# Four seven-product pairs instead of two in the gate and short-convolution blocks of a decoder trunk

## The chip, the cores and the metric

The kernel runs on one core of one Trainium2 chip. The metric is device time in microseconds (us) of one execution, here the median of three runs. All inputs and outputs are float32 in HBM.

## The reference

One layer of a hybrid decoder trunk, 256 tokens, width 2048. After a layer norm, one large projection feeds three token mixers and three gates; the mixers' outputs are projected, gated, summed, projected once more, and a SwiGLU FFN follows. Cut to what matters:

```
x = layer_norm(x, ln_in_g, ln_in_b)
z = einsum('bsd,de->bse', x, w_in)                      # 2048 -> 13312
a_b, a_c, a_h, b_u, b_v, c_a, c_g, g = split(z)         # seven of 1024, g of 3 x 2048
gates = sigmoid(g + gate_bias)
y_a = a_b * causal_conv(a_c * a_h, conv_a_w)            # 3 taps
y_b = chunked_spatial_gating(b_u, b_v, ...)
y_c = silu(layer_norm(causal_conv(c_a * sigmoid(c_g), cc_conv_w) + cc_conv_b))   # 31 taps
merged = sum_n gates[n] * (y_n @ w_branch[n])           # each 1024 -> 2048
x = layer_norm(alpha * x + merged @ w_out)
x = layer_norm(alpha * x + (silu(x @ w_g) * (x @ w_u)) @ w_ffn_out)
```

## The kernel before

**Precision.** Every float32 operand of a matrix product is split in two parts of a shorter format, `hi` (a cast on ScalarE, L127) and `lo` (the difference, on VectorE, L129). A *product* is three matmuls on TensorE, each of 128 x 128 weights and 512 moving columns: hi by hi, lo by hi, hi by lo (`product`, L236 to L238; in the chunk form L190 to L192).

**Weights.** All weight tiles stand in one list, `plan`, in the order of use: 128 rows by 1024 columns (or 256 rows by 512), 512 KB each. `pump` runs at the head of every step: it loads up to DMA_AHEAD tiles ahead into five raw buffers (`wraw`), splits up to SPLIT_AHEAD ahead (`split_one`) into the rings `whi` and `wlo` of SPLIT_BUFS = 7 buffers each, and pops two items of `background`, the list that holds the 248 taps of branch C's convolution (`tap`, L547 and L550). The framework that builds the program may put instructions of one engine into another order than the code's, as far as the data allow; on the chip each engine then runs its instructions in that fixed order.

**Blocks.** `gemm_block` makes 256 tokens by 1024 columns: two token halves by two column halves, four results in four PSUM banks. A step of kind "one" takes a tile of 128 rows through four products. A step of kind "pair" takes two tiles (2 by 2 sub-blocks b11, b12, b21, b22 of 128 x 512) through seven products instead of eight, after Strassen and Winograd: sums of the four token sub-blocks (`token_sums`, in `xTS`, `mTS`, `hS`) against sums of the four weight sub-blocks (`split_pair`: t1 = b11 + b12, t2 = t1 + b22, t3 = b12 + b22, t4 = t2 + b21). Four of the products gather in banks of their own (p1, p5, p6, p7) over all pairs of the block and are added to the results at the end (L281 to L285, then `total`, L644). While these banks are in use, deferred work that needs a bank waits (`run_deferred(held)`).

`add_block` lays out a block's steps: `lead` single tiles first (LEAD = 6, or all there are), then each pair followed by a share of the remaining singles. X_PAIRS = 2 is the number of pairs where the left side is the normalized input; H_PAIRS = 2 in the FFN's second product; S_PAIRS = 3 in the FFN's first.

**Order of the work.** Eight chunk products (branch C's input, branch B's input), then gate blocks `("g", n, b)` of 16 row tiles each followed by a branch product `("p", n, b)` of 8 single tiles; between branch B and branch A stand the three short-convolution blocks ac, ah, ab. So: gB0 pB0 gB1 pB1, ac ah ab, gA0 pA0 gA1 pA1, gC0 pC0 gC1 pC1, then the output block o0 (`("o", 0)`), two output chunks, and the FFN. The deferred tasks of ab (`later`, L755 on) run in the first steps of gA0; `finish_c`, which reads branch C's convolution, runs in gC0.

The pair's split, as it stands:

```
add(ts[:, 0, :], b11, b12)
add(b12, b12, b22)
add(ts[:, 1, :], ts[:, 0, :], b22)
second = split_tile(t1)
add(ts[:, 2, :], ts[:, 1, :], b21)
low = split_tile(ts[:, 0:2, :])
first = split_tile(t0)
last = split_tile(ts[:, 2:3, :], 1)
```

Of the kernel before, what the change touches and what calls it, by code (L numbers as in the profile page):

```python
# [24 lines left out]
NW = 512  # L25
KT = 2
RAW_BUFS = 5
SPLIT_BUFS = 7
DMA_AHEAD = 6
SPLIT_AHEAD = 3  # L30
DEFER = 2
# [7 lines left out]
S_PAIRS = 3  # L39
H_PAIRS = 2  # L40
SUMS_AT = 5
X_PAIRS = 2
LEAD = 6

OFF_AB, OFF_AC, OFF_AH = 0, DA, 2 * DA
OFF_BU, OFF_BV = 3 * DA, 4 * DA
OFF_CA, OFF_CG = 5 * DA, 6 * DA
OFF_G = 7 * DA
# [3 lines left out]
def trunk_kernel(ctx: ExitStack, tc: tile.TileContext, x, ln_in_g, ln_in_b, w_in, gate_bias,  # L52
                 conv_a_w, sg_ln_g, sg_ln_b, sg_w, sg_b, cc_conv_w, cc_conv_b, cc_ln_g, cc_ln_b,
                 w_branch, w_out, ln_mix_g, ln_mix_b, w_ffn_in, w_ffn_out, ln_ffn_g, ln_ffn_b, out):
    nc = tc.nc
# [27 lines left out]
    def blocks(ap):  # L83
        return ap.rearrange("p (b d) -> p b d", d=P)
# [11 lines left out]
    block = {}  # L96
    fast = set()

    def add_block(key, src, n0, kt0, nk, pairs=0):


        rest = nk - 2 * pairs
        lead = min(LEAD, rest)
        steps, k = [("one", 2 * pairs + q) for q in range(lead)], 2 * pairs + lead
        for i in range(pairs):
            steps.append(("pair", i))
            upto = 2 * pairs + lead + (rest - lead) * (i + 1) // pairs
# [14 lines left out]
    state = {"dma": 0, "split": 0}  # L122
    background = []

    def split_tile(t, n=KT):
        hi = wp.tile([P, KT, NW], F32R, name="whi")[:, 0:n, :]
        nc.scalar.copy(out=hi, in_=t)  # L127
        lo = wp.tile([P, KT, NW], F32R, name="wlo")[:, 0:n, :]
        nc.vector.tensor_tensor(out=lo, in0=t, in1=hi.bitcast(F32), op=ALU.subtract)  # L129
        return hi, lo  # L130

    def split_pair(t0, t1):


        b12, b11, b22, b21 = t0[:, 0, :], t0[:, 1, :], t1[:, 0, :], t1[:, 1, :]
        ts = wp.tile([P, 3, NW], F32, name="tsum", bufs=1)

        def add(out, a, b):
            nc.vector.tensor_tensor(out=out, in0=a, in1=b, op=ALU.add)  # L139

        add(ts[:, 0, :], b11, b12)
        add(b12, b12, b22)
        add(ts[:, 1, :], ts[:, 0, :], b22)
        second = split_tile(t1)
        add(ts[:, 2, :], ts[:, 1, :], b21)
        low = split_tile(ts[:, 0:2, :])
        first = split_tile(t0)
        last = split_tile(ts[:, 2:3, :], 1)

        def part(pair, i):  # L150
            return pair[0][:, i, :], pair[1][:, i, :]

        return {"b11": part(first, 1), "t3": part(first, 0), "b22": part(second, 0), "b21": part(second, 1),
                "t1": part(low, 0), "t2": part(low, 1), "t4": part(last, 0)}

    def split_one():
        j = state["split"]
# [75 lines left out]
    def product(ps, a, b, first, last):  # L233

        (ah, al), (bh, bl) = a, b
        nc.tensor.matmul(ps, lhsT=ah, rhs=bh, start=first, stop=False)  # L236
        nc.tensor.matmul(ps, lhsT=ah, rhs=bl, start=False, stop=False)  # L237
        nc.tensor.matmul(ps, lhsT=al, rhs=bh, start=False, stop=last)  # L238

    def gemm_block(key, xs, evac, combos=None, with_sums=None):  # L240

        steps = block[key]
        xh, xl = xs
        pairs = sum(kind == "pair" for kind, _, _ in steps)
        outs = {at: acc_bank() for at in ((0, 0), (1, 0), (0, 1), (1, 1))}
        adds, shared, free_at = {}, None, 0

        def a_of(k, t):
            return xh[:, k, cols(t, P)], xl[:, k, cols(t, P)]

        def c_of(i, c):
            return combos[0][:, c, i, :], combos[1][:, c, i, :]

        for s_, (kind, q, tile_) in enumerate(steps):
            pump(tile_)
            b = split_t.pop(tile_)
            first, last = s_ == 0, s_ == len(steps) - 1  # L260
            if kind == "one":
                hi, lo = b
                for i, ((t, n), ps) in enumerate(outs.items()):
                    product(ps, a_of(q, t), (hi[:, n, :], lo[:, n, :]), first, last)
                    if last:
                        evac(i, t, n, ps, adds.get((t, n)))
            else:
                if q == 0:
                    shared = [halves[1].tile([P, NW], F32, name="acc") for _ in range(4)]
                p1, p5, p6, p7 = shared  # L270
                st, sp = q == 0, q == pairs - 1
                product(outs[0, 1], a_of(2 * q + 1, 0), b["b21"], first, last)
                product(outs[0, 0], c_of(q, 3), b["b22"], first, last)
                product(p5, c_of(q, 0), b["t1"], st, sp)
                product(p6, c_of(q, 1), b["t2"], st, sp)
                product(p1, a_of(2 * q, 0), b["b11"], st, sp)
                product(p7, c_of(q, 2), b["t3"], st, sp)
                product(outs[1, 1], a_of(2 * q + 1, 1), b["t4"], first, last)
                if sp:
                    c1, u, r, v, w = (new_tmp() for _ in range(5))  # L280
                    nc.scalar.copy(out=c1, in_=p1)  # L281
                    nc.vector.tensor_tensor(out=u, in0=p6, in1=c1, op=ALU.add)
                    nc.vector.tensor_tensor(out=r, in0=p5, in1=u, op=ALU.subtract)
                    nc.vector.tensor_tensor(out=v, in0=u, in1=p7, op=ALU.subtract)
# [42 lines left out]

    def plan_branch(n):
        for b in range(2):
            add_block(("g", n, b), wi, OFF_G + n * D + 2 * b * NW, 0, 16, X_PAIRS)  # L330
            add_block(("p", n, b), w_branch[0, n], 2 * b * NW, 0, 8)

    for j in range(2):
# [4 lines left out]
            plan_in(nm, off, j)  # L338
    plan_branch(BR_B)
    for nm, off in (("ac", OFF_AC), ("ah", OFF_AH), ("ab", OFF_AB)):  # L340
        add_block(nm, wi, off, 0, 16, X_PAIRS)
    plan_branch(BR_A)
    plan_branch(BR_C)
    add_block(("o", 0), w_out[0], 0, 0, 16, X_PAIRS)
    for j in (2, 3):
        add_chunk(("o", j), w_out[0], j * NW, 0, 16)
    for f0, f1 in FF_PARTS:
# [87 lines left out]
    def token_sums(dst, q, y0, y1, n):  # L435


        a11, a12, a21, a22 = y0[:, 0:2 * n:2, :], y0[:, 1:2 * n:2, :], y1[:, 0:2 * n:2, :], y1[:, 1:2 * n:2, :]
        xa, xb = (new_tmp().rearrange("p (c b d) -> p c b d", c=2, d=P)[:, :, 0:n, :] for _ in range(2))
        x1, x2, x3, x4 = xa[:, 0], xa[:, 1], xb[:, 0], xb[:, 1]  # L440
        for o, p_, q_, op in ((x1, a21, a22, ALU.subtract), (x2, x1, a11, ALU.subtract),
                              (x3, a21, a11, ALU.subtract), (x4, a12, x2, ALU.add)):
            nc.vector.tensor_tensor(out=o, in0=p_, in1=q_, op=op)
        for c, o in ((0, xa), (2, xb)):
            h = dst[0][:, c:c + 2, q:q + n, :]
            nc.scalar.copy(out=h, in_=o)
            nc.vector.tensor_tensor(out=dst[1][:, c:c + 2, q:q + n, :], in0=o, in1=h.bitcast(F32), op=ALU.subtract)
# [2 lines left out]

    def new_sums():

        return tuple(act.tile([P, 4, H_PAIRS, P], F32R, name=f"sum{i}") for i in range(2))

    xTS = new_sums()
    x_kept = [blocks(xpool.tile([P, NW], F32, name=f"xk{t}")) for t in range(NT)]
    def x_stats(t):
        st = xpool.tile([P, 4, 6], F32, name=f"st{t}")
        for q in range(4):
# [3 lines left out]
    def x_norm(t, q):  # L463
        mu, rs = x_ms[t]
        norm_transposed(xT, q, t, xt[t][:, cols(q)], mu, rs, PR_ING, PR_INB, new_tmp(), act=ACT_BLOCKS[t],
                        y=x_kept[t] if q == 0 else None)

    x_ms = [x_stats(0)]
    x_norm(0, 0)
# [483 lines left out]
```

## Time and profile before

| | |
|---|---|
| median of three runs | 1538.31 us (1536.48 to 1538.59) |
| the profiled execution | 1535.72 us |
| its span, first to last instruction | 1533.7 us |
| TensorE matmuls | 1511.9 us busy, 6799 instructions |
| VectorE | 1343.7 us busy |
| ScalarE | 769.2 us busy |
| granted TensorE clock, mean | 0.997 of full speed |
| HBM | 304.8 MB read |

The profile is of one execution. PE is TensorE, DVE VectorE, ACT ScalarE, POOL GpSimd, SP the engine that issues the weight loads. A line such as L129 is that of the kernel's file, often of a helper, so the names of the tiles tell which work it is. Matmuls overlap: each shows 0.39 us, while one starts every 0.23 us, and a busy TensorE need not be at its peak. "Idle before" is time in which an engine did nothing in front of an instruction, put down to what released it.

### The profile page before, as it was taken

The numbers are of one execution on the slowest core, as the hardware profiler recorded it, in microseconds if no ns is written. First come the engines' busy times: TensorE is split into PE (matmuls) and PEld (weight loads), VectorE is DVE, ScalarE is ACT, GpSimd is POOL, SyncE is SP. The second block draws the span as 40 slices with busy tenths as digits, with TensorE's granted clock in tenths as the row PEclk, the third lists the DMA queues.
The fourth block names the chain that finished last, engine by engine and source line by source line (L and its number), as shares of the span: only waits on it lengthen the run. The fifth ranks groups of instructions, "written<-read, shape, count | busy, mean of one in ns | idle before, by whom it ended". The sixth has DMA issues, their size and how long they took to land.

```text
span 1533.7 us, 18857 instructions
## 1 busy us (share of the span) xinstructions
PE 1511.9 (99%) x6799; PEld 1246.5 (81%) x6799; DVE 1343.7 (88%) x1803; ACT 769.2 (50%) x885; POOL 35.6 (2%) x61
## 2 busy tenths in 40 slices
PE   7999999999999999999999999999999999999997
PEld 5888888888888888888887888888888888888885
DVE  7699999987789878879889899998899998899677
ACT  6544445544454554545436455554555554455551
POOL 0000000000000000000101000000000000000001
PEclk9999999999999999999999999999999999999999
DMA  7766657566665764757666657576665666666653
GB/s 238 260 189 184 190 161 237 161 217 200 206 188 167 240 202 154 271 169 235 227 210 185 211 188 222 180 243 198 189 194 178 205 207 205 197 201 195 217 187 129
DMA packets 102548, 308.14 MB, mean 201 GB/s; under 512 B 9908, under 2 KB 11028, under 8 KB 102454
## 3 DMA queue, kind: packets, MB, share of 16 engines
q1 hardware_dynamic: 98006, 293.29, 60.1%
q0 software_dynamic: 3520, 11.54, 2.6%
q10 hardware_dynamic: 928, 2.11, 0.4%
q8 instruction: 53, 0.87, 0.2%
q14 instruction: 41, 0.34, 0.1%
HBM read 304.80 MB, written 2.10 MB: 200 GB/s over the span
## 4 chain that ended last, share of the span: by engine, by line
PE 86%; DVE 9%; issue 3%; ACT 1%; DMA 1%; POOL 0%; DVEq 0%; POOLq 0%; ACTq 0%
PE acc L236 24%; PE acc L238 24%; PE acc L237 24%; DVE cv L550 4%; PE acc L190 4%; PE acc L192 4%; PE acc L191 4%; DVE wlo L129 2%; PE acc L298 1%; DMA x<-in_x_dram 0%; DVE tmp L628 0%; DMA wraw<-in_w_in_dram 0%; DVE st L460 0%; DVE tl L305 0%; ACT whi L127 0%
## 5 line engine op out<-in xcount | busy, mean ns | idle before, releaser
L127 ACT CAST whi<-wraw 128x1024 fp32r<-128x1024 f32 x552 | 576.2, 1052 | 515.6 <-PE acc L238 268.4
L129 DVE TENSOR_TENSOR wlo<-wraw,whi 128x1024 fp32r<-128x1024 f32 x552 | 665.5, 1218 | 113.8 <-ACT whi L127 106.2
L236 PE MATMUL acc<-whi,th 128*128 128x512 f32 x1235 | 484.1, 392 | 0.0
L238 PE MATMUL acc<-whi,tl 128*128 128x512 f32 x1235 | 481.0, 390 | 0.0
L237 PE MATMUL acc<-wlo,th 128*128 128x512 f32 x1235 | 480.6, 389 | 0.0
L238 PEld LDWEIGHTS acc<-whi,tl 128*128 128x128 f32 x1235 | 231.8, 188 | 48.6
L237 PEld LDWEIGHTS acc<-wlo,th 128*128 128x128 f32 x1235 | 232.0, 188 | 47.2
L236 PEld LDWEIGHTS acc<-whi,th 128*128 128x128 f32 x1235 | 231.9, 188 | 46.9
L190 PE MATMUL acc<-whi,th 128*128 128x512 f32 x496 | 194.7, 393 | 2.1 <-ACT th L304 2.1
L192 PE MATMUL acc<-whi,tl 128*128 128x512 f32 x496 | 193.7, 391 | 0.0
L191 PE MATMUL acc<-wlo,th 128*128 128x512 f32 x496 | 193.5, 391 | 0.0
L127 ACT CAST whi<-tsum 128x1024 fp32r<-128x1024 f32 x114 | 95.3, 836 | 158.4 <-DVE tsum L139 93.0
L129 DVE TENSOR_TENSOR wlo<-tsum,whi 128x1024 fp32r<-128x1024 f32 x114 | 108.7, 953 | 22.3 <-ACT whi L127 21.9
L190 PEld LDWEIGHTS acc<-whi,th 128*128 128x128 f32 x496 | 93.3, 188 | 21.7 <-ACT th L304 2.7
L192 PEld LDWEIGHTS acc<-whi,tl 128*128 128x128 f32 x496 | 93.3, 188 | 19.9 <-DVE tl L305 0.6
L191 PEld LDWEIGHTS acc<-wlo,th 128*128 128x128 f32 x496 | 93.5, 188 | 19.6 <-DVE wlo L129 0.7
L550 DVE SCALAR_TENSOR_TENSOR cv<-pad,cw,cv 128x256 f32<-128x256 f32 x240 | 101.2, 476 | 0.0
L139 DVE TENSOR_TENSOR tsum<-tsum,wraw 128x512 f32<-128x512 f32 x114 | 78.1, 685 | 1.0
L236 PE MATMUL acc<-whi,yh 128*128 128x512 f32 x192 | 75.2, 392 | 0.0
L238 PE MATMUL acc<-whi,yl 128*128 128x512 f32 x192 | 74.8, 389 | 0.0
L237 PE MATMUL acc<-wlo,yh 128*128 128x512 f32 x192 | 74.7, 389 | 0.0
L644 DVE TENSOR_TENSOR tmp<-acc,tmp 128x512 f32<-128x512 f32 x92 | 59.7, 682 | 0.4
(162 smaller groups left out, 1167.8 us busy)
## 6 DMA issues: line engine op xcount, KB each, us to landing
wraw<-in_w_in_dram SPq DMA_DIRECT2D x208, 512.0 KB, 4.3
wraw<-in_w_ffn_in_dram SPq DMA_DIRECT2D x176, 512.0 KB, 4.3
wraw<-in_w_ffn_out_dram SPq DMA_DIRECT2D x88, 512.0 KB, 4.7
wraw<-in_w_branch_dram SPq DMA_DIRECT2D x48, 512.0 KB, 5.0
wraw<-in_w_out_dram SPq DMA_DIRECT2D x32, 512.0 KB, 5.4
tmp<-in_gate_bias_dram POOLq DMA_DIRECT2D x12, 256.0 KB, 4.5
R<-in_x_dram POOLq DMA_DIRECT2D x8, 256.0 KB, 8.6
x<-in_x_dram SPq DMA_DIRECT2D x2, 512.0 KB
```

Of the source, the lines that this page charges most:

```text
L127: nc.scalar.copy(out=hi, in_=t)
L129: nc.vector.tensor_tensor(out=lo, in0=t, in1=hi.bitcast(F32), op=ALU.subtract)
L139: nc.vector.tensor_tensor(out=out, in0=a, in1=b, op=ALU.add)
L190: nc.tensor.matmul(ps, lhsT=xh[:, k, ts], rhs=hi[:, kk, :], start=first, stop=False)
L191: nc.tensor.matmul(ps, lhsT=xh[:, k, ts], rhs=lo[:, kk, :], start=False, stop=False)
L192: nc.tensor.matmul(ps, lhsT=xl[:, k, ts], rhs=hi[:, kk, :], start=False, stop=last)
L236: nc.tensor.matmul(ps, lhsT=ah, rhs=bh, start=first, stop=False)
L237: nc.tensor.matmul(ps, lhsT=ah, rhs=bl, start=False, stop=False)
L238: nc.tensor.matmul(ps, lhsT=al, rhs=bh, start=False, stop=last)
L298: nc.tensor.transpose(out=tp[:, b, :], in_=src[:, b, :], identity=ident)
L550: nc.vector.scalar_tensor_tensor(out=cv[:, b, :], in0=pad[:, b, q:q + S], scalar=w_, in1=cv[:, b, :], op0=ALU.mult, op1=ALU.add)
L644: nc.vector.tensor_tensor(out=c, in0=ps, in1=add, op=ALU.add)
```

## The change

X_PAIRS goes from 2 to 4: each of the six gate blocks and ac, ah, ab has four pairs and eight single tiles. The output block stays at two (it takes H_PAIRS now). `add_block` gets a lead of its own: the gate blocks with b = 1, and ac and ah, have LEAD_G = 4 single tiles and then four times a pair and a single; the gate blocks with b = 0 and ab keep six, so that the order there is six singles, two pairs, a single, two pairs, a single.

The sums of a pair are made in place: `tsum` is one row of 512 instead of three, t2 and t4 are written over b22 and b21 once these are split, and t1 gets a small split of its own (`thi`, `tlo`, one buffer each). SPLIT_BUFS goes from 7 to 6. The order of the seven products changes so that t2, t4 and t1 come last. The token sums have room for four pairs; those of the input are made in two calls, one step apart.

```diff
-SPLIT_BUFS = 7
+SPLIT_BUFS = 6
-X_PAIRS = 2
+X_PAIRS = 4
+LEAD_G = 4
...
-        ts = wp.tile([P, 3, NW], F32, name="tsum", bufs=1)
+        ts = wp.tile([P, NW], F32, name="tsum", bufs=1)
...
-        add(ts[:, 0, :], b11, b12)
+        add(ts, b11, b12)
         add(b12, b12, b22)
-        add(ts[:, 1, :], ts[:, 0, :], b22)
         second = split_tile(t1)
-        add(ts[:, 2, :], ts[:, 1, :], b21)
-        low = split_tile(ts[:, 0:2, :])
         first = split_tile(t0)
-        last = split_tile(ts[:, 2:3, :], 1)
+        add(b22, ts, b22)
+        add(b21, b22, b21)
+        low = split_tile(t1)
+        hi = wp.tile([P, NW], F32R, name="thi", bufs=1)
+        nc.scalar.copy(out=hi, in_=ts)
+        lo = wp.tile([P, NW], F32R, name="tlo", bufs=1)
+        nc.vector.tensor_tensor(out=lo, in0=ts, in1=hi.bitcast(F32), op=ALU.subtract)
...
-                product(p5, c_of(q, 0), b["t1"], st, sp)
-                product(p6, c_of(q, 1), b["t2"], st, sp)
                 product(p1, a_of(2 * q, 0), b["b11"], st, sp)
                 product(p7, c_of(q, 2), b["t3"], st, sp)
+                product(p6, c_of(q, 1), b["t2"], st, sp)
                 product(outs[1, 1], a_of(2 * q + 1, 1), b["t4"], first, last)
+                product(p5, c_of(q, 0), b["t1"], st, sp)
...
-            add_block(("g", n, b), wi, OFF_G + n * D + 2 * b * NW, 0, 16, X_PAIRS)
+            add_block(("g", n, b), wi, OFF_G + n * D + 2 * b * NW, 0, 16, X_PAIRS, LEAD_G if b else LEAD)
...
-        add_block(nm, wi, off, 0, 16, X_PAIRS)
+        add_block(nm, wi, off, 0, 16, X_PAIRS, LEAD if nm == "ab" else LEAD_G)
...
-    add_block(("o", 0), w_out[0], 0, 0, 16, X_PAIRS)
+    add_block(("o", 0), w_out[0], 0, 0, 16, H_PAIRS)
...
-        return tuple(act.tile([P, 4, H_PAIRS, P], F32R, name=f"sum{i}") for i in range(2))
+        return tuple(act.tile([P, 4, X_PAIRS, P], F32R, name=f"sum{i}") for i in range(2))
...
-    defer(lambda: token_sums(xTS, 0, x_kept[0], x_kept[1], X_PAIRS), SUMS_AT, False)
-    defer(more_params, SUMS_AT + 1)
+    for q in range(2):
+        defer(lambda q=q: token_sums(xTS, 2 * q, x_kept[0][q], x_kept[1][q], 2), SUMS_AT + q, False)
+    defer(more_params, SUMS_AT + 2)
```

## Rows read from the trace of the kernel before

**Rows 1.** The page's first part: busy time, share of the span, instructions.

```profile
PE 1511.9 (99%) x6799; PEld 1246.5 (81%) x6799; DVE 1343.7 (88%) x1803; ACT 769.2 (50%) x885; POOL 35.6 (2%) x61
```

**Rows 2.** Timeline of PE: start us, length us, engine, line, operation, tiles.

```profile
251.09 0.39 PE L236 MATMUL acc<-whi,yh 128*128 128x512 f32 x1
...
251.77 0.39 PE L236 MATMUL acc<-whi,yh 128*128 128x512 f32 x1
```

**Rows 3.** Waits of PE, longest first: us in total, times, longest us.

```profile
PE acc L298 <- DVE tmp L419: 6.6, 4, 2.7
```

**Rows 4.** Windows, blocks gB0 to gA0: stretch, its us, busy by engine, clock, DMA.

```profile
202.90:248.40 45.50, 45.23 (x212) 37.42 (x211) 45.50 (x78) 21.81 (x24) 0.55 (x1) 1.00 0.58 182
248.40:271.00 22.60, 22.60 (x105) 18.82 (x104) 21.59 (x33) 11.49 (x14) 1.09 (x2) 1.00 0.71 237
271.00:313.20 42.20, 42.20 (x188) 34.93 (x187) 42.07 (x67) 20.39 (x21) 0.00 (x0) 1.00 0.58 180
313.20:334.90 21.70, 21.70 (x97) 18.00 (x96) 18.72 (x28) 10.71 (x12) 0.00 (x0) 1.00 0.66 216
334.90:377.10 42.20, 42.20 (x187) 34.92 (x187) 31.71 (x35) 20.37 (x21) 0.00 (x0) 1.00 0.65 200
377.10:419.30 42.20, 42.20 (x188) 34.95 (x187) 32.96 (x37) 20.26 (x21) 0.00 (x0) 1.00 0.64 199
419.30:464.10 44.80, 44.80 (x211) 37.16 (x210) 39.56 (x54) 22.99 (x26) 0.00 (x0) 1.00 0.62 195
464.10:508.30 44.20, 44.20 (x206) 36.59 (x205) 42.88 (x64) 23.05 (x27) 2.16 (x4) 1.00 0.60 193
```

**Rows 5.** Windows of L550 alone (DVE): a chunk with taps, and block pB1.

```profile
90.40:112.20 21.80, 13.32 (x32) 1.00 0.66 194
...
313.20:334.90 21.70, 2.55 (x6) 1.00 0.66 216
```

**Rows 6.** Timeline of DVE in pB0: four subtractions in a row.

```profile
251.88 4.63 DVE L129 TENSOR_TENSOR wlo<-wraw,whi 128x1024 fp32r<-128x1024 f32 x4
```

**Rows 7.** Timeline of DVE before the end of gA0 at 508.3.

```profile
496.70 3.93 DVE L129 TENSOR_TENSOR wlo<-wraw,whi 128x1024 fp32r<-128x1024 f32 x3 [0.21 <-ACT whi L127]
...
501.47 1.23 DVE L129 TENSOR_TENSOR wlo<-wraw,whi 128x1024 fp32r<-128x1024 f32 x1 [0.23 <-ACT whi L127]
...
504.41 2.35 DVE L129 TENSOR_TENSOR wlo<-wraw,whi 128x1024 fp32r<-128x1024 f32 x2
506.67 1.28 DVE L644 TENSOR_TENSOR tmp<-acc,tmp 128x512 f32<-128x512 f32 x2
507.87 1.28 DVE L675 TENSOR_TENSOR gate<-tmp 128x512 f32<-128x512 f32 x2
```

**Rows 8.** Windows, blocks pA0, gA1, pA1, gC0, columns as in Rows 4.

```profile
508.30:530.00 21.70, 21.70 (x97) 18.00 (x96) 16.79 (x20) 10.53 (x12) 1.07 (x2) 1.00 0.72 234
530.00:572.20 42.20, 42.20 (x187) 34.92 (x187) 32.72 (x38) 20.36 (x21) 0.00 (x0) 1.00 0.62 191
572.20:594.00 21.80, 21.80 (x98) 18.05 (x97) 16.33 (x20) 10.52 (x12) 0.00 (x0) 1.00 0.63 204
594.00:637.90 43.90, 43.90 (x204) 36.59 (x203) 40.71 (x54) 24.66 (x29) 1.07 (x2) 1.00 0.62 197
```

**Rows 9.** Groups by form: ScalarE's cast of a pair's sums; busy us, mean ns.

```profile
L127 ACT CAST whi<-tsum 128x1024 fp32r<-128x1024 f32 x57 | 60.0, 1053 | 135.6 <-DVE tsum L139 90.8 <-PE acc L238 33.8 <-DVE wlo L129 3.3
```

**Rows 10.** Windows of DVE in two FFN blocks, fg2 and fu2.

```profile
903.90:947.30 43.40, 42.10 (x55) 1.00 0.56 177
947.30:989.10 41.80, 40.96 (x53) 1.00 0.67 205
```

**Rows 11.** The page's DMA issues: count, KB each, us to landing.

```profile
wraw<-in_w_in_dram SPq DMA_DIRECT2D x208, 512.0 KB, 4.3
```

**Rows 12.** Windows, the second gemm (ca0), columns as in Rows 4.

```profile
46.00:67.70 21.70, 21.70 (x97) 18.00 (x96) 12.28 (x11) 10.90 (x11) 0.00 (x0) 1.00 0.90 304
```

More of the change, by code (lines that the diff above doesn't have):

```diff
@@ L97, in trunk_kernel, with add_block @@
     fast = set()
-    def add_block(key, src, n0, kt0, nk, pairs=0):
+    def add_block(key, src, n0, kt0, nk, pairs=0, lead=LEAD):
         rest = nk - 2 * pairs
-        lead = min(LEAD, rest)
+        lead = min(lead, rest)
         steps, k = [("one", 2 * pairs + q) for q in range(lead)], 2 * pairs + lead
@@ L123, in trunk_kernel, with split_tile @@
     background = []
-    def split_tile(t, n=KT):
-        hi = wp.tile([P, KT, NW], F32R, name="whi")[:, 0:n, :]
+    def split_tile(t):
+        hi = wp.tile([P, KT, NW], F32R, name="whi")
         nc.scalar.copy(out=hi, in_=t)
-        lo = wp.tile([P, KT, NW], F32R, name="wlo")[:, 0:n, :]
+        lo = wp.tile([P, KT, NW], F32R, name="wlo")
         nc.vector.tensor_tensor(out=lo, in0=t, in1=hi.bitcast(F32), op=ALU.subtract)
@@ L153, in split_pair @@
         return {"b11": part(first, 1), "t3": part(first, 0), "b22": part(second, 0), "b21": part(second, 1),
-                "t1": part(low, 0), "t2": part(low, 1), "t4": part(last, 0)}
+                "t1": (hi, lo), "t2": part(low, 0), "t4": part(low, 1)}
     def split_one():
@@ L451, in new_sums @@
     def new_sums():
-        return tuple(act.tile([P, 4, H_PAIRS, P], F32R, name=f"sum{i}") for i in range(2))
+        return tuple(act.tile([P, 4, X_PAIRS, P], F32R, name=f"sum{i}") for i in range(2))
     xTS = new_sums()
-    x_kept = [blocks(xpool.tile([P, NW], F32, name=f"xk{t}")) for t in range(NT)]
+    x_kept = [[blocks(xpool.tile([P, NW], F32, name=f"xk{t}{q}")) for q in range(2)] for t in range(NT)]
     def x_stats(t):
@@ L465, in x_norm @@
         norm_transposed(xT, q, t, xt[t][:, cols(q)], mu, rs, PR_ING, PR_INB, new_tmp(), act=ACT_BLOCKS[t],
-                        y=x_kept[t] if q == 0 else None)
+                        y=x_kept[t][q] if q < 2 else None)
     x_ms = [x_stats(0)]
```

## The prediction

> **What bounds the kernel now.** I read the engines' shares first [rows 1]: TensorE 99%, VectorE 88%, ScalarE 50%. A busy TensorE proves little by itself, so the second view is its matmuls in order of time: the first matmul of one product starts at 251.09 and that of the next at 251.77 [rows 2], so a product (three matmuls of 512 columns) costs 0.68 us. The third view is what TensorE waits for [rows 3]: the longest entry is 6.6 us in four waits, all in the opening normalization. Between 203 and 1522 us TensorE simply runs product after product. The end is set by the number of products, as long as VectorE delivers.
>
> So the fourth view asks how near VectorE is to not delivering, block by block [rows 4]. In the order of the rows the blocks are gB0, pB0, gB1, pB1, ac, ah, ab, gA0 (g a gate block, p the branch product behind it, 0 and 1 the column halves). VectorE is busy 45.50 of 45.50 us in gB0 and 42.07 of 42.20 in gB1, and 42.88 of 44.20 in gA0. Part of this is the convolution taps of branch C (L550). The code pops two at each step, 16 in a chunk of eight steps; the rows show 32 in such a chunk [rows 5], so ready taps are drawn forward into VectorE's free time. They are exhausted in pB1, where the last six run [rows 5]. That cushion ends there; it isn't free time, for the taps have to be done.
>
> **The change, part by part.**
>
> *Products.* Two more pairs in each of nine blocks (six gate blocks, ac, ah, ab): each pair does seven products where two single tiles do eight. 9 x 2 x 0.68 = 12.2 us off TensorE, 1.36 a block. The output block keeps its two pairs, the FFN its own numbers.
>
> *What a pair costs VectorE.* Four subtractions of 1024 run back to back in 4.63 us [rows 6]: (4.63 - 1.22) / 3 = 1.137 us from start to start. Two of 512 start at 506.67 and the next pair of them at 507.87 [rows 7]: 0.60 each. A single tile needs one subtraction, 1.137. A pair needs four additions, three subtractions of 1024 and one of 512: 4 x 0.60 + 3 x 1.137 + 0.60 = 6.41. The new split_pair has the same count. Replacing four singles by two pairs adds 2 x (6.41 - 2.27) = 8.28 us of VectorE to a block and takes 1.36 us of TensorE from it.
>
> *Does it fit?* From gB0 to the end of gA0 the eight rows [rows 4] give 305.4 us with VectorE busy 45.50 + 21.59 + 42.07 + 18.72 + 31.71 + 32.96 + 39.56 + 42.88 = 275.0. Six of the blocks get pairs: 275.0 + 49.7 = 324.7 us of work. TensorE would want only 305.4 - 8.2 = 297.2. An operation that stands alone shows 1.22 where the row of four shows 1.137, so closer packing gives back 0.08 each; in pB1, ac, ah and ab there are 154 operations [rows 4], and if a third of them stand alone that is 4 us. Work is 320.7, short by 23.5.
>
> *How much may be late.* In front of 202.9 VectorE is already full of taps (32 per chunk, [rows 5]), so nothing can be done earlier. At the end of gA0 (508.3) it is ahead of TensorE: five tiles of the next block were subtracted by then (the last two of the three at 496.70, then 501.47 and the two at 504.41) and three operations of gA0's own evacuation were done (506.67 to 508.3) [rows 7]. All but the first tile could come later: 4 x 1.137 + 3 x 0.60 = 6.3 us. What is left, 23.5 - 6.3 = 17.2 us, TensorE must wait, mostly in ab and gA0, when the cushion of taps has turned into a debt.
>
> *Behind gA0* [rows 8] (pA0, gA1, pA1, gC0): with the additions 16.8 + 41.0 + 16.3 + 49.0 = 123.1 us of VectorE against 21.7 + 40.8 + 21.8 + 42.5 = 126.8 of TensorE. It fits, with 3.7 us over: no more waiting, and no debt repaid that would shorten anything. gC1 is like gA1.
>
> *A new wait inside the pair.* The sum t4 is now made in b21's place, and t2, t4 are cast together as `low`. So the last addition on VectorE, ScalarE's cast and VectorE's subtraction follow one another, and the cast takes 1.05 us [rows 9]; with the two hand-overs about 1.15 us in which VectorE, in order, does what else stands ready or nothing. Before, the subtraction of the other tile and an addition stood there. In the stretch above there are 24 pairs: from 0 to 27.6 us. I take it as filled where taps remain (16 pairs in gB0, gB1, ac, ah) and half filled in ab and gA0 (8 pairs), nearest to the row of gA0 above, where hardly any time was free but other work was always queued: 8 x 1.15 / 2 = 4.6 us.
>
> *The same wait in the FFN and the output blocks.* Three pairs a block, up to 3.5 us. The fullest neighbours are 42.10 of 43.40 and 40.96 of 41.80 [rows 10]: 2.1 us free, 6.9 needed at worst, 4.8 late, under the 6.3 that may be late. I take 0; ends 0 and 5.
>
> *Buffers.* Six split buffers for seven: the lead on single tiles falls by one tile, 4 x 0.68 = 2.72 us; a pair now holds three and a small one of its own instead of four. That costs nothing where VectorE is late anyway; up to 1 us in each of four blocks (gB0, ab, gA0, gC0) where two pairs follow each other and the second's t1 waits for the last product of the first (thi, tlo have one buffer). Behind that cast stand the casts of the next tile on ScalarE and their subtractions on VectorE. Ends 0 and 4; I take 0, since the lead is used up there by the debt above. A raw tile is held to the end of its pair. A load needs 4.3 us from issue [rows 11], and between the end of one pair and the need for the fifth tile on, VectorE has a pair or more to do, 6.41: hidden; if VectorE were faster it would cost the difference.
>
> *Start.* A second call of token_sums adds six operations of at most 512 elements to VectorE, at most 6 x 0.60 = 3.6 us, and two casts to ScalarE, due in the first gemm; more_params comes one step later. In the second gemm VectorE is busy 12.28 of 21.70 [rows 12]: hidden there, at worst 3.6.
>
> **The sum.** To the end of gA0: -8.2 + 17.2 = +9.0; three further blocks -4.1; the wait in the pairs +4.6; together +9.5 us. The profiled execution took 1535.7 us (span 1533.7), which gives 1545; the median of the runs is 2.6 above it, so 1548.
>
> A rule speaks still more against the change. The rows show an operation starting 0.08 us before the one in front has ended (1.137 against 1.22). The Trainium skill, "VectorE: DVE Perf Modes", section "The DRAIN you can't avoid", says that the next operation does not start until the pipe has emptied, and to keep the number of operations low. By that a pair would cost its full durations, 4 x 0.68 + 3 x 1.22 + 0.68 = 7.1 us (0.68 is 1.28 - 0.60 in [rows 7]), the six blocks 55 instead of 49.7, and the time 1554. The rows decide for the smaller price; the larger lies in the range.
>
> **Rivals.**
>
> *The taps slip behind gA0.* Nobody reads branch C's convolution before gC0. If the order lets single tiles and pairs go first, the debt is carried over pA0 and pA1, which have 5 us free each. Then the account closes at gC0: 23.5 less the 3.7 free there and some 3 of packing, less 6.3, is a wait of 10.5 and -12.2 + 10.5 = -1.7: 1536 to 1537, a little less if the wait in the pairs is filled throughout. It decides if at least 7 us of taps (some 17) run behind 508. For it: taps were moved freely before. Against: two are popped at each step, and by the middle of gA0 all are due. Chance 0.2.
>
> *VectorE holds.* All 12.2 us come: 1526. It would need 17 us of work less in the stretch than the rows give. Chance 0.08.
>
> *The wait in the pairs is bare.* If nothing stands between the last addition and the subtraction of `low`, 24 x 1.15 = 27.6 instead of 4.6: 1571, slower for certain. It decides from the order on VectorE within a pair: any wait on ScalarE in front of `low`'s subtraction that is over 1 us each time. Against it: in the rows of gA0 other tiles' subtractions stand between a pair's own. Chance 0.12.
>
> **How the numbers follow.** The forecast, VectorE bound from gB1 to gA0 with the waits mostly filled, has 0.6: 1548, between 1541 and 1556. A measurement of this kernel can tell about 0.2%, 3.1 us. Faster: 0.08 and a third of 0.2, 0.14. Same, 1535.2 to 1541.4: the rest of that rival and a tenth of the forecast, 0.2. Slower: 0.66. The range leaves out the full gain and part of the bare wait: 1532 to 1567.
>
> **What would show it.** Right: TensorE, which never waited in these blocks, waits for VectorE's `wlo` in ab and gA0, some 17 to 22 us in all, while VectorE's busy share from 203 to 515 is 97% or more; gate blocks of branch A's second half are about 41 us, shorter than before. Taps (L550) reach beyond pB1. Wrong: TensorE's products keep 0.68 us through gA0, or taps run far behind it (first rival), or VectorE shows over 1 us idle in front of every `low` (third). The sum falls if the packing gives back much more than 4 us.

## The result, and the profile after

The changed kernel takes 1552.7 us in the median (1550.7 to 1553.8), the kernel before 1538.4 beside it: a ratio of 1.010, 95% interval 1.0087 to 1.0113. It is slower by 14.3 us. The forecast was 1548 with a range of 1532 to 1567.

The profiled execution took 1553.8 us (span 1552.1) against 1535.7 (span 1533.7). Line numbers move a little: the cast is L128, the split's subtraction L130, the pair's additions L140, the small split `thi`, `tlo` L150 and L152, a product L240 to L242, the taps L555.

First the page's first part, to be held against [rows 1], and the head of its fourth, the chain that ended last by engine:

```profile
PE 1515.7 (98%) x6745; PEld 1234.2 (80%) x6745; DVE 1417.3 (91%) x1917; ACT 794.7 (51%) x923; POOL 33.8 (2%) x61
...
PE 58%; DVE 30%; issue 7%; DMA 3%; ACT 1%; POOL 0%; DVEq 0%; SPq 0%; ACTq 0%; POOLq 0%
```

The same chain before the change:

```profile
PE 86%; DVE 9%; issue 3%; ACT 1%; DMA 1%; POOL 0%; DVEq 0%; POOLq 0%; ACTq 0%
```

TensorE has 54 matmuls less, as the change promises, and yet its busy time rose: a matmul shows 0.39 us where one can start every 0.23, so a short wait leaves no idle time. The chain shows the waits: VectorE carries 30% of it, where it was 9% before.

The windows of the same blocks as in [rows 4] and [rows 8], gB0 to gC0 (stretch, its length, busy time of PE, PEld, DVE, ACT and POOL, granted clock, DMA share, GB/s):

```profile
203.90:249.20 45.30, 44.48 (x205) 35.98 (x205) 45.30 (x75) 22.25 (x25) 0.55 (x1) 1.00 0.47 145
249.20:271.60 22.40, 22.10 (x97) 17.95 (x97) 20.07 (x26) 11.47 (x13) 1.09 (x2) 1.00 0.81 271
271.60:314.90 43.30, 42.37 (x190) 34.48 (x189) 43.30 (x62) 23.44 (x27) 0.00 (x0) 1.00 0.53 170
314.90:336.60 21.70, 21.70 (x97) 18.00 (x96) 20.94 (x29) 12.10 (x14) 0.00 (x0) 1.00 0.76 276
336.60:378.00 41.40, 41.13 (x181) 33.72 (x181) 41.39 (x60) 21.12 (x23) 0.00 (x0) 1.00 0.52 166
378.00:419.50 41.50, 41.41 (x181) 33.41 (x180) 41.18 (x53) 21.55 (x25) 0.00 (x0) 1.00 0.61 196
419.50:467.80 48.30, 45.24 (x198) 34.40 (x197) 48.30 (x72) 24.90 (x29) 0.00 (x0) 1.00 0.55 173
467.80:521.20 53.40, 47.55 (x205) 34.79 (x204) 51.30 (x74) 25.61 (x30) 1.09 (x2) 1.00 0.54 166
521.20:544.30 23.10, 22.24 (x99) 18.05 (x98) 22.09 (x32) 13.01 (x15) 2.16 (x4) 1.00 0.75 264
544.30:585.10 40.80, 40.80 (x181) 33.80 (x180) 39.35 (x48) 21.25 (x24) 0.00 (x0) 1.00 0.59 182
585.10:606.90 21.80, 21.80 (x98) 18.04 (x97) 18.45 (x23) 12.22 (x15) 0.00 (x0) 1.00 0.80 287
606.90:652.50 45.60, 43.98 (x198) 35.00 (x197) 44.42 (x61) 24.86 (x30) 1.07 (x2) 1.00 0.46 145
```

ab (the seventh) takes 48.30 us, VectorE busy in all of it; TensorE alone would want 44.8 - 1.4 = 43.4. gA0 takes 53.40 instead of 42.8. gA1 takes 40.80, the full gain. From gB0 to the end of gA0 the eight rows add to 317.3 us, with VectorE busy 311.8, 98%; before it was 305.4.

What TensorE and its weight loads wait for in that stretch (us in total, times, longest us). Before, TensorE waited once in these blocks, for 0.3 us:

```profile
PE acc L240 <- ACT whi L128: 6.6, 13, 1.2
PE acc L241 <- DVE wlo L130: 2.9, 7, 0.8
PE acc L240 <- ACT thi L150: 1.3, 1, 1.3
...
PEld acc L240 <- ACT whi L128: 13.5, 17, 1.7
PEld acc L241 <- DVE wlo L130: 9.1, 17, 1.1
```

Most of it is put down to ScalarE's cast, but ScalarE is busy half the time. What it waits for itself is the pair's addition on VectorE:

```profile
ACT whi L128 <- DVE wraw L140: 71.2, 31, 5.2
```

Before, it mostly waited for TensorE to free a split buffer (107.2 us in 89 waits). The second entry after the change, 19.9 us in 14 waits, is for loads of raw tiles, and the load queue itself waits for a buffer that one of VectorE's subtractions frees (266.7 of its 273.5 us of waits). So these chains lead back to VectorE, 98% busy.

### The profile page after: what moved, and what is told of

It is laid out like the page before. It is cut to its first block, busy times and chain, and to the rows that moved or that the text cites. A ratio compares the mean times of both kernels' runs of the same rounds, so it can differ in the third digit from the quotient of the medians.

```text
span 1552.1 us, 18910 instructions
## 1 busy us (share of the span) xinstructions
PE 1515.7 (98%) x6745; PEld 1234.2 (80%) x6745; DVE 1417.3 (91%) x1917; ACT 794.7 (51%) x923; POOL 33.8 (2%) x61
## 4 chain that ended last, share of the span: by engine, by line
PE 58%; DVE 30%; issue 7%; DMA 3%; ACT 1%; POOL 0%; DVEq 0%; SPq 0%; ACTq 0%; POOLq 0%
PE acc L241 15%; PE acc L242 15%; PE acc L240 15%; DVE wlo L130 11%; DVE cv L555 6%; PE acc L195 4%; PE acc L194 4%; PE acc L196 4%; DVE wraw L140 3%; DMA wraw<-in_w_in_dram 2%; DMA wraw<-in_w_out_dram 1%; DVE tmp L649 1%; PE acc L302 1%; DVE tsum L140 1%; ACT whi L128 1%
## 5 line engine op out<-in xcount | busy, mean ns | idle before, releaser
L128 ACT CAST whi<-wraw 128x1024 fp32r<-128x1024 f32 x627 | 647.1, 1052 | 619.8 <-DVE wraw L140 192.8
L130 DVE TENSOR_TENSOR wlo<-wraw,whi 128x1024 fp32r<-128x1024 f32 x627 | 751.1, 1218 | 89.8 <-ACT whi L128 83.2
L240 PE MATMUL acc<-whi,th 128*128 128x512 f32 x1145 | 448.0, 393 | 3.0 <-ACT whi L128 2.7
L241 PE MATMUL acc<-wlo,th 128*128 128x512 f32 x1145 | 446.4, 390 | 1.5 <-DVE wlo L130 1.4
L242 PE MATMUL acc<-whi,tl 128*128 128x512 f32 x1145 | 446.2, 390 | 0.7 <-DVE tl L309 0.7
L240 PEld LDWEIGHTS acc<-whi,th 128*128 128x128 f32 x1145 | 214.5, 188 | 50.3 <-ACT whi L128 7.8
L241 PEld LDWEIGHTS acc<-wlo,th 128*128 128x128 f32 x1145 | 215.1, 188 | 47.9 <-DVE wlo L130 3.5
L242 PEld LDWEIGHTS acc<-whi,tl 128*128 128x128 f32 x1145 | 214.9, 188 | 45.6 <-DVE tl L309 1.1
L194 PE MATMUL acc<-whi,th 128*128 128x512 f32 x496 | 195.5, 396 | 2.9 <-ACT th L308 2.9
L195 PE MATMUL acc<-wlo,th 128*128 128x512 f32 x496 | 194.7, 394 | 1.4 <-DVE wlo L130 1.2
L196 PE MATMUL acc<-whi,tl 128*128 128x512 f32 x496 | 194.7, 393 | 0.0
L194 PEld LDWEIGHTS acc<-whi,th 128*128 128x128 f32 x496 | 93.9, 190 | 23.2 <-ACT th L308 3.9
L140 DVE TENSOR_TENSOR wraw<-wraw 128x512 f32<-128x512 f32 x150 | 102.9, 686 | 8.0 <-DMA wraw<-in_w_out_dram 3.7
L555 DVE SCALAR_TENSOR_TENSOR cv<-pad,cw,cv 128x256 f32<-128x256 f32 x240 | 103.3, 475 | 0.0
L242 PE MATMUL acc<-whi,yl 128*128 128x512 f32 x192 | 74.7, 390 | 0.0
L240 PE MATMUL acc<-whi,yh 128*128 128x512 f32 x192 | 73.4, 392 | 0.0
L150 ACT CAST thi<-tsum 128x512 fp32r<-128x512 f32 x75 | 46.4, 618 | 41.8 <-DVE tsum L140 31.7
L240 PE MATMUL acc<-whi,sum 128*128 128x512 f32 x144 | 57.1, 397 | 5.5 <-ACT whi L128 5.5
L140 DVE TENSOR_TENSOR tsum<-wraw 128x512 f32<-128x512 f32 x75 | 51.3, 685 | 9.6 <-DMA wraw<-in_w_ffn_out_dram 3.4
```

Source lines behind the costliest of these rows:

```text
L150: nc.scalar.copy(out=hi, in_=ts)
L194: nc.tensor.matmul(ps, lhsT=xh[:, k, ts], rhs=hi[:, kk, :], start=first, stop=False)
L195: nc.tensor.matmul(ps, lhsT=xh[:, k, ts], rhs=lo[:, kk, :], start=False, stop=False)
L196: nc.tensor.matmul(ps, lhsT=xl[:, k, ts], rhs=hi[:, kk, :], start=False, stop=last)
L555: nc.vector.scalar_tensor_tensor(out=cv[:, b, :], in0=pad[:, b, q:q + S], scalar=w_, in1=cv[:, b, :], op0=ALU.mult, op1=ALU.add)
```

## The experiments

Two readings stood against each other. One, the forecast's, does a sum over a whole stretch: VectorE's work from gB0 to gA0 against TensorE's. The other says that work can't be moved that far, so that each block, with its neighbour at most, must pay for itself. Besides these the rework itself (in-place sums, fewer buffers), the taps, and the couples of pairs in gB0, ab, gA0 and gC0 were suspects. All ratios are to the kernel before.

### The rework without the pairs

```diff
-X_PAIRS = 4
-LEAD_G = 4
+X_PAIRS = 2
+LEAD_G = 6
...
-    for q in range(2):
-        defer(lambda q=q: token_sums(xTS, 2 * q, x_kept[0][q], x_kept[1][q], 2), SUMS_AT + q, False)
-    defer(more_params, SUMS_AT + 2)
+    defer(lambda: token_sums(xTS, 0, x_kept[0][0], x_kept[1][0], X_PAIRS), SUMS_AT, False)
+    defer(more_params, SUMS_AT + 1)
```

> Two pairs a block as before, with everything else of the change: sums in place, t1 in a small split of its own, six split buffers, the new order of products. If the number of pairs is the cause (VectorE's debt), the time stays near that of before, 1538 to 1543: at most the raw tiles held longer show, in the start and in the output block, where the changed kernel lost some 1 and 4 us. If the rework of the pair is the cause (its wait between the last addition and the subtraction of low, two of seven rings less), most of the 14 us stays: 1546 or more.

1537.3 us, ratio 1.0003 (0.9994 to 1.0013). Sums in place, six buffers and the new order of the products cost nothing as a whole; only the FFN's first block takes 26.9 us instead of 25.1, here as in all that have the rework (26.8 to 27.2). The 14 us come with the number of pairs.

### Three pairs

```diff
-X_PAIRS = 4
+X_PAIRS = 3
```

(The second call of the token sums then makes one sum instead of two.)

> Three pairs in each of the nine blocks, the rest as in the changed kernel. Debt theory: to the end of gA0 the six blocks add 6 x 4.14 = 24.9 us to VectorE's 275.0, less 4 of packing 295.9, and TensorE has 305.4 - 4.1 = 301.3: it fits, so the nine products saved show, 6.1 us, less up to 5 for the rework: 1532 to 1537. Rival, each added pair costs by its own wait: half of the change's loss, about 1545.

1533.2 us, ratio 0.9978 (0.9969 to 0.9987): faster than both. The third pair still pays, the fourth costs. The windows of ab and gA0, columns as above:

```profile
416.30:459.70 43.40, 43.40 (x201) 35.92 (x199) 41.30 (x57) 23.69 (x27) 0.00 (x0) 1.00 0.57 187
459.70:505.40 45.70, 44.88 (x209) 36.65 (x208) 45.04 (x68) 23.12 (x28) 3.06 (x4) 1.00 0.52 166
```

gA0, the fuller one, already waits: 45.70 where TensorE wants 43.5.

### Half the taps, after and before

In the first kernel every second of the 248 taps is left out of the changed kernel, in the second the same of the kernel before; branch C's convolution is then not the reference's.

```diff
-            for q in range(KC):
+            for q in range(0, KC, 2):
                 for b in range(4):
                     background.append(lambda q=q, b=b: tap(q, b))
```

> The changed kernel with every second tap row of branch C's 31-tap convolution left out (120 of 248 taps, 120 x 0.395 = 47 us of VectorE), so the output differs in that branch. Debt theory: the debt of 23.5 us is gone, TensorE keeps its pace through gA0 and the 12.2 us of saved products show against the same cut of the kernel before: 1526 to 1533. Rival, the wait within the pairs or the buffers: the taps don't matter, 1545 or more.

> The kernel before with the same 120 taps left out (the output differs in that branch). TensorE is its bound and the taps filled VectorE's free time only: both theories expect 1536 to 1539, no change that can be told.

The changed kernel comes to 1543.2 us, 1.0039 (1.0026 to 1.0052); the kernel before stays, 0.9997 (0.9987 to 1.0006). The taps carry 9 of the 14 us, and the kernel before has none to gain from them. But I had expected the whole 12 us of the products, and that failed. Windows gB0, ah, ab, gA0:

```profile
203.10:246.70 43.60, 43.60 (x205) 36.36 (x205) 36.69 (x48) 22.12 (x26) 0.55 (x1) 1.00 0.48 152
372.70:413.50 40.80, 40.80 (x181) 33.80 (x180) 39.01 (x46) 22.73 (x25) 0.00 (x0) 1.00 0.59 190
413.50:462.30 48.80, 45.31 (x197) 34.38 (x196) 47.62 (x74) 22.99 (x28) 0.00 (x0) 1.00 0.45 150
462.30:509.30 47.00, 44.69 (x197) 34.58 (x196) 44.99 (x57) 25.04 (x29) 1.07 (x2) 1.00 0.57 189
```

With half the taps gone, the rest are done before gB0: none runs in this stretch. gB0 then has 6.9 us of VectorE free (36.7 of 43.6 busy) and ah, at full rate, 1.8, and yet the next block, ab, is 5.4 us late and gA0 4.2. By the stretch's sum it fits: the kernel before had 37.5 us of taps in the stretch, and 275.0 - 37.5 + 49.7 = 287.2 stands against 297.2 of TensorE. Free time in front was of no use to ab. That speaks for the block's account.

### Four pairs in ab and gA0 alone

This decides between the two sums. It starts from the changed kernel, with the number of pairs set block by block:

```diff
+PAIRS_AT = {("g", 1, 0): 2, ("g", 1, 1): 2, "ac": 2, "ah": 2, "ab": 4, ("g", 0, 0): 4, ("g", 0, 1): 2,
+            ("g", 2, 0): 2, ("g", 2, 1): 2}
...
-            add_block(("g", n, b), ..., X_PAIRS, LEAD_G if b else LEAD)
+            add_block(("g", n, b), ..., PAIRS_AT["g", n, b], LEAD_G if b and PAIRS_AT["g", n, b] == 4 else LEAD)
...
-        add_block(nm, wi, off, 0, 16, X_PAIRS, LEAD if nm == "ab" else LEAD_G)
+        add_block(nm, wi, off, 0, 16, PAIRS_AT[nm], LEAD_G if PAIRS_AT[nm] == 4 else LEAD)
```

A block with two or three pairs so has a lead of six, and ab with four pairs a lead of four and a single behind each pair, unlike in the changed kernel. The other kernels with `PAIRS_AT` have this edit too and differ in the table.

> The changed kernel with four pairs in ab and gA0 alone, two in the other seven blocks: 4 products less than before, 2.7 us of TensorE. Two ways to do the sum. Over the whole stretch gB0 to gA0, as the prediction did it: VectorE's work is 275.0 + 2 x 8.28 = 291.6 us against 302.7 of TensorE, it fits, TensorE does not wait, and the time is 0.998 of before. Block by block, since work can't be done many tiles ahead of its use: ab and gA0 hold 39.6 + 42.9 + 16.6 = 99.1 us of VectorE in 43.5 + 42.8 = 86.3 of TensorE, 12.8 short, of which 6.3 may be late, so 6 to 7 us of wait in ab and gA0 together, some of the late work carried into gC0, and the time is 3 to 5 us over before, 1.002 to 1.0035.

1542.6 us, ratio 1.0035 (1.0021 to 1.0048). The stretch's sum, by which it fits with 11 us over, is refuted. ab, gA0, pA0:

```profile
418.50:462.00 43.50, 43.50 (x204) 36.05 (x204) 43.01 (x59) 24.38 (x28) 0.00 (x0) 1.00 0.52 169
462.00:512.70 50.70, 46.77 (x199) 35.84 (x198) 49.54 (x74) 25.27 (x30) 3.20 (x4) 0.97 0.48 160
512.70:534.50 21.80, 21.80 (x98) 18.04 (x97) 19.08 (x23) 11.48 (x13) 1.07 (x2) 1.00 0.82 277
```

ab itself doesn't wait. It needs 39.6 + 8.3 = 47.9 us of VectorE and gets 43.0, so 4.9 us of its work run in gA0. There they meet 51.2 us of gA0's own, and gA0 is 7.9 us late (50.7 against 42.8). In front of ab, ah has its 9 us of VectorE free, unused. About 1.5 us of the 7.9 are the clock (last section).

### Two pairs in ab and gA0, four elsewhere

```diff
+PAIRS_AT = {("g", 1, 0): 4, ("g", 1, 1): 4, "ac": 4, "ah": 4, "ab": 2, ("g", 0, 0): 2, ("g", 0, 1): 4,
+            ("g", 2, 0): 4, ("g", 2, 1): 4}
```

> Four pairs everywhere but in ab and gA0, which keep two: fourteen added pairs. Debt theory: 271 + 4 x 8.28 = 304 us of VectorE against 300 of TensorE up to gA0, 4 short, less than the 6.3 that may be late: no wait there. 9.5 us of products saved, less 3 for gC0, 2.7 for the output block and 1.8 for the first FFN product: 0.998 to 1.001 of the time before. Rival, each pair costs its own wait: 14/18 of the change's loss, ratio 1.007.

1540.9 us, 1.0026 (1.0015 to 1.0037), slightly above what I expected. 10 of the 14 us are gone, but ab with its two pairs is still full (VectorE busy 45.29 of 45.30), and gC0 waits as after the change:

```profile
419.80:465.10 45.30, 44.73 (x204) 36.34 (x203) 45.29 (x68) 24.06 (x27) 0.00 (x0) 1.00 0.62 202
594.90:640.20 45.30, 44.03 (x197) 34.92 (x196) 44.02 (x60) 24.97 (x30) 1.07 (x2) 1.00 0.46 149
```

### Pairs where there is room

Four pairs where a block had over 9 us of VectorE free (ac, ah, gA1, gC1), three in gB1, whose taps can move, and in gC0 with 3 us free, two elsewhere. The second kernel adds a third pair in ab and drops that of gC0; the third one has four in gC0.

```diff
+PAIRS_AT = {("g", 1, 0): 2, ("g", 1, 1): 3, "ac": 4, "ah": 4, "ab": 2, ("g", 0, 0): 2, ("g", 0, 1): 4,
+            ("g", 2, 0): 3, ("g", 2, 1): 4}
```

> Pairs where VectorE has room: gB0 2, gB1 3, ac 4, ah 4, ab 2, gA0 2, gA1 4, gC0 3, gC1 4 (ten more than before instead of eighteen). Debt theory: up to gA0 five pairs add 5 x 4.14 = 20.7 us to 271, TensorE has 302: it fits, and gA1, gC0, gC1 fit by themselves. Ten products are saved, 6.8 us, less the 1.8 that the first FFN product lost with the rework alone: 0.9963 to 0.998 of the time before, some 1531 to 1533 beside 1536.3. Rival, every added pair costs: slower than three pairs in all blocks.

> The pairs by room once more, with a third pair in ab (41.5 us of VectorE in 44.1 there with two) and the third of gC0 taken out again: gB0 2, gB1 3, ac 4, ah 4, ab 3, gA0 2, gA1 4, gC0 2, gC1 4. Ten pairs more than before, as in the first such kernel, 6.8 us of TensorE. If each block pays for itself, ab loses 0.7 less 0.3 and gA0, the next one, takes over up to 1 us of late work; gC0 is back at 43.9: the same as the first such kernel within 1 us, 0.996 to 0.9975 of before.

> The first kernel with pairs by room (gB0 2, gB1 3, ac 4, ah 4, ab 2, gA0 2, gA1 4, gC0 3, gC1 4), with one thing changed: gC0 has four pairs instead of three, 0.7 us of TensorE less. If a block must pay for itself, gC0 (42.5 us of VectorE in 43.7 with three) waits: 45 to 46 us. If the loss of the output blocks o0 and o2 is late work carried on from gC0, they are 45 to 46 and 22.3 to 23.3 us instead of 44.4 and 21.9, and the time is 3 to 5 us above that kernel, 0.9985 to 1.000 of before. If that loss comes from somewhere else (four pairs in gC1, or ab and gA0), o0 and o2 stay, and the time is 1 to 2 us above that kernel, 0.997 to 0.998.

The first takes 1531.5 us, ratio 0.9965 (0.9954 to 0.9977), the lowest of all, though its interval overlaps that of three pairs in every block (0.9969 to 0.9987): ten pairs more than before are worth 6.8 us, and 5.6 arrive. Its ab and gA0:

```profile
417.60:461.70 44.10, 44.10 (x203) 36.44 (x202) 41.53 (x58) 22.70 (x26) 0.00 (x0) 1.00 0.61 212
461.70:506.60 44.90, 44.90 (x211) 37.34 (x210) 43.71 (x65) 23.01 (x27) 2.41 (x4) 1.00 0.58 196
```

The third pair in ab costs about 4 us: 1535.5, 0.9990 (0.9980 to 0.9999), which I had not expected. ab is shorter, but gA0 takes 48.90, and here VectorE is not full:

```profile
460.00:508.90 48.90, 46.26 (x212) 37.03 (x211) 44.67 (x66) 22.73 (x28) 2.16 (x4) 1.00 0.54 182
```

In its trace the first pair of gA0 has its first addition at 469.10 and its last at 481.58, with ab's late work between; its raw tiles stay occupied as long. ScalarE then waits 5.1 us for a load, and VectorE with it. One entry of ScalarE's waits in gA0 (us in total, times, longest us; the other two of the three waits stand before that pair), then three rows of VectorE's timeline:

```profile
ACT whi L130 <- DMA wraw<-in_w_in_dram: 8.5, 3, 5.1
```

```profile
469.10 0.68 DVE L142 TENSOR_TENSOR tsum<-wraw 128x512 f32<-128x512 f32 x1
...
481.58 0.68 DVE L142 TENSOR_TENSOR wraw<-wraw 128x512 f32<-128x512 f32 x1
...
491.35 0.69 DVE L142 TENSOR_TENSOR wraw<-wraw 128x512 f32<-128x512 f32 x1 [0.88 <-DMA wraw<-in_w_in_dram]
```

That the held tile is the reason is my reading of these rows; a sixth raw buffer would test it, and no run has one. The block's account alone doesn't give this loss: with three pairs in ab and three in gA0 as well, gA0 took only 45.70.

The fourth pair in gC0 also costs 4 to 5 us: 1536.1, 0.9993 (0.9984 to 1.0003). gC0 is 45.7 us instead of 43.7, as expected of a block that must pay for itself. Behind it, with gC1 at its full rate of 40.8 between, o0 is 44.8 instead of 44.4, less than the 45 to 46 expected, and o2 22.6 instead of 21.9. With two pairs in gC0, in the second kernel, they take 44.0 and 21.8, as before the change. So a part of what o0 and o2 lose after the change goes with the pairs in gC0, three blocks earlier, in one trace each. That it is late work carried on is not shown: VectorE is busy only 40.3 of the 44.8 us of o0.

### Pairs apart

Here gB0, ab, gA0 and gC0 also get a lead of four and a single between any two pairs.

```diff
-            add_block(("g", n, b), ..., X_PAIRS, LEAD_G if b else LEAD)
+            add_block(("g", n, b), ..., X_PAIRS, LEAD_G)
...
-        add_block(nm, wi, off, 0, 16, X_PAIRS, LEAD if nm == "ab" else LEAD_G)
+        add_block(nm, wi, off, 0, 16, X_PAIRS, LEAD_G)
```

> The changed kernel with a lead of four singles in all nine blocks, so that no two pairs follow each other without a single between them (the changed kernel has two such couples in gB0, ab, gA0, gC0, the blocks that wait most). Debt theory: the work is the same, so at most 1 us a block comes back: ratio 1.007 to 1.011. Rival, the couples are the cause (t1 of the second waits for the first's last product, single buffer): ab, gA0 and gC0 give back most of 4.9 + 10.6 + 3.1 us: ratio below 1.002.

1551.8 us, 1.0095 (1.0080 to 1.0110): as after the change. ab is 48.8, gA0 53.2 us. The couples are not the main cause, which would have brought 12 us or more. Up to some 3 us could be hidden: the granted clock was 0.97 in both blocks here, 1.00 after the change, and such a fall costs about 1.5 us (last section).

### Taps popped more slowly

```diff
-        for _ in range(min(BACKGROUND, len(background))):
+        for _ in range(min(pops[0], len(background))):
...
+    pops[0] = 1
     gemm_block("ac", xT, evac_ac, xTS)
```

(`pops` starts at BACKGROUND.)

> The changed kernel, but from ac on one tap instead of two is popped at each step, so that the taps are due later and may slip behind gA0 (branch C reads them in gC0). Debt theory: the debt is carried into pA0 to pA1, where VectorE has 1 to 5 us free a block; ab and gA0 lose up to 6 us less and gA1 or pA1 up to 3 more: 3 to 6 us faster than the changed kernel, a ratio of about 1.006 to 1.008 to the kernel before. If the place of the taps is of no matter: 1.010 as the change.

1556.7 us, 1.0129 (1.0114 to 1.0144), more than either theory allowed, and not a test of what I meant. The taps did not move. The windows of their line alone, ab and gA0, show six and five of them, as after the change:

```profile
418.70:467.00 48.30, 2.69 (x6) 1.00 0.54 174
467.00:519.60 52.60, 2.28 (x5) 0.97 0.52 169
```

So the step that pops a tap doesn't decide where the framework puts it. What moved is the task behind the taps, branch C's layer norm, which now falls into gC0: VectorE's work there rises from 44.4 to 48.1 us and gC0 from 45.6 to 51.2. It shows the price of 4 us of work more in a full block, with some 1.5 us of clock in it (0.97 in gC0), and nothing of taps carried over.

## Why the prediction was right, and where not

**VectorE as the bound from gB1 to gA0: right, in size too.** The stretch is 11.9 us longer; -8.2 + 17.2 + 4.6 = 13.6 was forecast. VectorE was busy for 311.8 us of it and idle for 5.5, where the sum had 297.2 + 17.2 = 314.4 and 4.6. TensorE's loss is 317.3 - 297.2 = 20.1 us against 21.8, at 98% busy. It lies in gB0 with 1.2, gB1 2.5, ac and ah 1.2 together, ab 4.9 and gA0 10.6.

**The size was right partly by luck.** The sum was taken over the stretch as if work could move anywhere in it. It can't: in gA0 and ab alone, 47.9 + 51.2 us of VectorE stood against 86.3 of TensorE. That the two sums agree here is due to the taps. They can run at any time, and filled the early blocks up to ah. With half the taps left out none runs in the stretch, the early blocks have time, and ab and gA0 are late all the same, by 9.6 us. What keeps a block's work from being done earlier, the six split buffers, the five raw ones or the order of the instructions, no run separates.

**The wait inside the pair: too large in the sum, 4.6 for 1.1.** VectorE's own waits for the cast in the stretch are 4.2 us in four, but that this is near 4.6 is chance. Three of the four, 3.1 us, stand in pB0 and pB1, which have no pairs and take no longer than before. One stands inside a pair, at the end of gA0, with nothing left to put between. The group of waits, then VectorE's timeline (start, length, in brackets the idle time before), the three and the one:

```profile
DVE wlo L130 <- ACT whi L128: 4.2, 4, 2.3
```

```profile
265.59 1.22 DVE L130 TENSOR_TENSOR wlo<-wraw,whi 128x1024 fp32r<-128x1024 f32 x1 [2.33 <-ACT whi L128]
...
327.88 1.22 DVE L130 TENSOR_TENSOR wlo<-wraw,whi 128x1024 fp32r<-128x1024 f32 x1 [0.36 <-ACT whi L128]
...
329.90 1.23 DVE L130 TENSOR_TENSOR wlo<-wraw,whi 128x1024 fp32r<-128x1024 f32 x1 [0.40 <-ACT whi L128]
...
513.12 0.68 DVE L140 TENSOR_TENSOR wraw<-tsum,wraw 128x512 f32<-128x512 f32 x1
513.72 0.68 DVE L152 TENSOR_TENSOR tlo<-tsum,thi 128x512 fp32r<-128x512 f32 x1
514.32 0.68 DVE L140 TENSOR_TENSOR wraw<-wraw 128x512 f32<-128x512 f32 x1
516.12 3.50 DVE L130 TENSOR_TENSOR wlo<-wraw,whi 128x1024 fp32r<-128x1024 f32 x3 [1.11 <-ACT whi L128]
```

1.11 us, the price of the third rival (1.15), but in one pair rather than 24. The third rival is false.

**"Behind gA0 no more waiting": wrong, by about 10 us, and with it the profiled sum (1545; it was 1554).** From the end of gA0 to the end of the FFN's first block the change costs 5.8 us where it was to bring 4.1. The step put pA0, gA1, pA1 and gC0 into one sum with 3.7 us over. gC0's own 49.0 against 42.5 stood in it, and the free time of the blocks ahead doesn't help gC0. It takes 45.60, 3.1 too much. pA0 and pC0, right behind gA0 and gC0, lose 1.8. o0 and o2 lose 2.7; of this some 1.6 goes with gC0's pairs, for from two to four of them there o0 went from 44.0 to 44.8 and o2 from 21.8 to 22.6. What makes the rest of it is open. The FFN's first block, below, is another 1.8.

**Buffers at 0: right for the rework alone, and yet a load is late in o0.** "Hidden" was said of the raw tile that is held to the end of its pair. In o0 VectorE waits for a load in the middle of a pair, with nothing else to do:

```profile
764.83 0.69 DVE L140 TENSOR_TENSOR wraw<-wraw 128x512 f32<-128x512 f32 x1 [3.70 <-DMA wraw<-in_w_out_dram]
```

The cover named there, a pair of VectorE work before the tile is needed, was missing. But the buffers alone don't make this wait: the rework without the pairs has the same six buffers, the same held tiles and the same two pairs in o0, its longest wait of this kind there is 1.1 us, and o0 takes 44.0 us, as before. What delays the load after the change isn't shown.

**The FFN at 0, from 0 to 5: 1.8,** in its first block, and the rework alone shows it. What in the rework makes it stays open. **Start at 0:** the stretch in front of gB0 is 1.0 us longer, but the opening chunk took 32.0 to 34.0 us in kernels with the same opening, so that is scatter.

**First rival, taps behind gA0: false.** The last run in gA0, none behind it (the taps' line, ab, gA0, pA0):

```profile
419.50:467.80 48.30, 2.70 (x6) 1.00 0.55 173
467.80:521.20 53.40, 2.30 (x5) 1.00 0.54 166
521.20:544.30 23.10, 0.00 (x0) 1.00 0.75 264
```

**The second rival** fell with the first wait. **The rule on the emptying pipe** would have put the sum nearer to the measured time (1554), but not by its own reason. Operations still start 0.60 us apart at 0.68 shown (513.12, 513.72, 514.32 above). The Trainium skill, "VectorE: DVE Perf Modes", section "The DRAIN you can't avoid", has the next one start only when the pipe is empty, and adds what the prediction left out, that an operation that is not held starts earlier. The trace after agrees with the addition, and the missing time lay elsewhere, behind gA0.

**Signs.** TensorE was to wait for `wlo`; it waits for `whi` more often (6.6 us in 13 waits against 2.9 in 7). The first matmul of a product reads `whi`, and its cast, too, waits for VectorE's additions. gA1 at about 41 us was right.

## What to carry to other kernels

When a second engine is nearly full, make its account block by block, each with the few microseconds that may run late into the next one; free time earlier counts only for work that may run at any time, such as the taps here, and free time later not at all. Then spend the trade block by block as well: ten extra pairs placed by room brought 5.6 us, nine spread evenly 3.2, and eighteen spread evenly cost 14. Even such an account can miss by microseconds: of the 5.6 us, 4 were lost when one pair was moved from gC0 to ab. A figure that fits over a long stretch is no proof that it fits in its fullest block.

## What the runs showed of the hardware

A matmul that follows a wait costs more than the wait. In gA0 after the change (TensorE, start, length):

```profile
489.39 0.50 PE L240 MATMUL acc<-whi,th 128*128 128x512 f32 x1 [1.22 <-ACT whi L128]
489.73 0.40 PE L240 MATMUL acc<-whi,sum 128*128 128x512 f32 x1
```

It shows 0.50 us instead of 0.39, and the next starts 0.34 us after it instead of 0.23; so it is, with 0.33 or 0.34, behind 22 of the 23 waits of 0.1 us or more from gB0 on. And the clock may follow. Near the end of gA0, in the kernel with four pairs in ab and gA0 alone, TensorE had been busy 0.66 and 1.38 of two stretches of 2 us. Then the granted clock fell to half, 1.2 of 2.4 GHz, and matmuls started 0.43 us apart for 3 us. The windows of TensorE (stretch, length, busy, clock, DMA share, GB/s), then its timeline:

```profile
504.00:506.00 2.00, 0.66 (x3) 1.00 0.75 229
506.00:508.00 2.00, 1.38 (x4) 0.95 0.08 33
508.00:510.00 2.00, 2.00 (x6) 0.50 0.59 221
```

```profile
508.01 0.63 PE L243 MATMUL acc<-wlo,sum 128*128 128x512 f32 x1
508.44 0.63 PE L244 MATMUL acc<-whi,sum 128*128 128x512 f32 x1
```

Eight matmuls at 0.43 instead of 0.23 cost about 1.5 us. In the profiled execution of the changed kernel the clock stayed at 1.00 in all the blocks shown, though gA0 took longer. What decides it isn't shown. It is not the length of one wait alone: with the pairs apart the clock stayed at 1.00 in pB0 behind a wait of 1.6 us, and with the taps popped more slowly it fell in gA0, where the longest was 1.4.
